# A modulation vector on four column strips of TensorE: norm1's part and g1 first, the rest in the course of the attention

## The chip, the cores and the metric

The kernel runs on one core of a Trainium2 chip. Its engines work side by side: TensorE (PE; its weight loads are listed as PEld), VectorE (DVE), ScalarE (ACT), GpSimd (POOL) and SyncE (SP, which here only issues DMAs). The metric is the device time of one execution in microseconds, lower is better. Times are given as the median of several runs, and one execution was recorded by the hardware profiler.

## The reference

One decoder layer over 1024 positions of width 1024. A vector c is turned into six rows of 1024 numbers, which shift, scale and gate the two sub-layers:

```python
c_act = jax.nn.silu(c)
mod = c_act @ ada_w[l] + ada_b[l]            # (1, 1024) @ (1024, 6144)
sh1, sc1, g1, sh2, sc2, g2 = jnp.split(mod, 6, axis=-1)
h = _rmsnorm(x, norm1_g[l]) * (1 + sc1) + sh1
p = h @ w_in[l]                              # q, k, v and u, 512 columns each
# q, k: RMS norm per head; 8 heads of 64, strictly causal stick-breaking attention
# u: 32 groups of a complex-diagonal state-space model (S5), gelu, GLU
o = concat(_rmsnorm(o_attn, attn_out_g[l]), _rmsnorm(o_ssm, ssm_out_g[l]))
x = x + g1 * (o @ w_out[l])
h = _rmsnorm(x, norm2_g[l]) * (1 + sc2) + sh2
up = causal_conv3(h @ ffn_w_up[l])           # width 2 * 2816
x = x + g2 * ((gelu(gate) * val) @ ffn_w_down[l])
```

The product with `ada_w` is a vector times a matrix of 1024 x 6144 in float32 (25 MB). It is what this change is about. Nothing else of the computation changes.

## The kernel before

The program is written out in full by Python loops, one instruction after another; a planner then orders each engine's instructions by a simulated timeline, so that instructions of one stage can stand between those of another, but each engine and each DMA queue then works strictly in the order given. Large products in float32 are done as three matmuls on rounded high and low halves (`hi`, `lo`).

Stages, in order:

1. norm1 and u (lines 141 to 238). For each of eight blocks k of 128 features, `load_k` fetches 1 MB of `ada_w` (the shift and the scale columns of that block, `ada_raw`) and the weights of u. The block's shift S1c and scale A1 come from the modulation; then x is transposed block by block on TensorE (line 233), ScalarE applies A1 and S1c (line 235), and `u_mm` adds the block to the projection of u. Five of its eight output tiles run inside the loop, the other three behind it (line 415). The modulation of block 0 is 16 matmuls with one column each (line 212); that of the other blocks is eight multiply-adds on VectorE over 256 columns (lines 215 to 217), whose 128 partitions a matmul with a column of ones then sums (line 220).
2. S5 and the projections of q, k and v (lines 412 to 650). `ssm_batch` runs four times between tiles of `proj`. Weight chunks of q, k and v are loaded and split by ScalarE and POOL (`load_wchunk`), into buffers which the chunk before must have left. `ada_back` (lines 560 to 583) computes six half rows of the modulation (g1, sh2, sc2), each with eight loads of 128x512 and eight multiply-adds on VectorE (line 569), and a sum over partitions on TensorE (line 573 or 577). It is a generator: `ada_step(3)` at line 601 advances it by three loads before each projection tile, and what is left is drained at line 649 behind the projection of v.
3. Attention (`head`, lines 679 to 726). Scores on TensorE (lines 697 to 700), two sigmoids on ScalarE (701, 702), a running product on VectorE (703), a product on POOL (705), transposes on TensorE (710), copies (714, 715) and the product with v (720, 721). Between the tiles, `after_tile` advances a second generator, `fillers`, at places given by the list `marks`, as shares of the heads' total weight: it prepares `w_out` (`wout_tile`, which multiplies by g1), and from mark 0.13 to 0.68 runs the output projection of the S5 half for eight row tiles (`ssm_out`, lines 795 to 799, a load of x, 24 matmuls and a store each). The buffers of `psM` in PSUM are shared by these. The last two heads run side by side when the fillers are done.
4. norm2 and the up projection (lines 894 to 1146), in 22 column blocks m; each `up_pair` is 84 matmuls of 512 columns. `g2_rows` computes a quarter of g2 behind each of the blocks 6 to 9, with eight loads and eight operations on VectorE each. g2 lies in the row that g1 had.
5. The down projection (lines 1158 to 1204), where the result is multiplied by g2.

The constants `ones` and `c_sb` (silu(c), one column per block of 128 inputs) are made at the start. All loads named here are issued from SP's queue.

Of the kernel before, what the change touches and what calls it, by code (L numbers as in the profile page):

```python
# [35 lines left out]
def hybrid_layer_kernel(  # L36
# [23 lines left out]
    def tt(eng, out, a, b, op):  # L60
        eng.tensor_tensor(out=out, in0=a, in1=b, op=op)  # L61
# [25 lines left out]
    cols_sb = const.tile([128, 32], F32, name="cols_sb")  # L87
    sp.dma_start(out=cols_sb, in_=cols)
    c_raw, n1g_sb, sh1b, sc1b = [cols_sb[:, 8 * i:8 * i + 8] for i in range(4)]
    cols2_sb = const.tile([128, 194], F32, name="cols2_sb")  # L90
    n2g_sb, outg_sb = cols2_sb[:, 0:8], cols2_sb[:, 8:16]
    cw_sb = cols2_sb[:, 16:148].rearrange("p (i m) -> p i m", i=3)
    cb_sb = cols2_sb[:, 148:192]
    gq_sb, gk_sb = cols2_sb[:, 192:193], cols2_sb[:, 193:194]

    ident = const.tile([128, 128], F32, name="ident")
    make_identity(nc, ident)
# [17 lines left out]
    o_d = dram.tile([512, 8, 128], F32, name="o_d")  # L115
    qk_d = dram.tile([2, 2, 512, 1024], F32, name="qk_d")
    x1_d = dram.tile([1024, 1024], F32, name="x1_d")
    x2_d = dram.tile([1024, 1024], F32, name="x2_d")
    a_d = dram.tile([NM * 128, 1024], F32, name="a_d")
    v_d = dram.tile([1024, 8, 128], F32, name="v_d")  # L120
# [80 lines left out]
    for k in range(NK):  # L201
        if k:
            load_k(k)
        if k == 1:
            sp.dma_start(out=cols2_sb, in_=cols2)
        raw = ada_raw[k]

        mps = psU.tile([128, 512], F32, tag="mps", name="mps", bufs=1)
        if k == 0:
            for i in range(2):  # L210
                for r in range(8):
                    pe.matmul(mps[:, i:i + 1], lhsT=raw[:, r, i * 128:(i + 1) * 128], rhs=c_sb[:, r:r + 1], start=(r == 0), stop=(r == 7))
        else:
            acc = pn.tile([128, 256], F32, tag="ada_acc", name="ada_acc1")
            dve.tensor_scalar(out=acc, in0=raw[:, 0, :], scalar1=c_sb[:, 0:1], scalar2=None, op0=MUL)
            for r in range(1, 8):
                stt(acc, raw[:, r, :], c_sb[:, r:r + 1], acc, MUL, ADD)
            for i in range(2):
                cs_ = slice(i * 128, (i + 1) * 128)
                pe.matmul(mps[:, i:i + 1], lhsT=acc[:, cs_], rhs=ones[:, 0:1], start=True, stop=True)  # L220
        tt(dve, S1c[:, k:k + 1], mps[:, 0:1], sh1b[:, k:k + 1], ADD)
        stt(A1[:, k:k + 1], mps[:, 1:2], sc1b[:, k:k + 1], n1g_sb[:, k:k + 1], ADD, MUL)
# [334 lines left out]

    TB, ZB, MB = 3, 2, 2

    def ada_back(ix):  # L560

        kind, o = divmod(ix * 512, 1024)
        acc = wp.tile([128, 512], F32, tag="uF", name="ada_acc", bufs=3)
        pool.memset(acc, 0.0)
        sp.dma_start(out=acc[0:1, :], in_=ada_br[ix:ix + 1, :])
        for r in range(8):
            raw = wp.tile([128, 512], F32, tag="uF", name="ada_raw", bufs=3)
            sp.dma_start(out=raw, in_=ada_r[ix, :, r])
            stt(acc, raw, c_sb[:, r:r + 1], acc, MUL, ADD)
            yield  # L570
        ps = psA.tile([128, 512], F32, tag="aux", name="adps")
        if kind == 0:
            pe.matmul(ps, lhsT=ones, rhs=acc, start=True, stop=True)
            act.activation(out=g1row[:, o:o + 512], in_=ps, func=AF.Copy)
        else:
            for j in range(4):
                pe.matmul(ps[:, j:j + 1], lhsT=acc[:, j * 128:(j + 1) * 128], rhs=ones[:, 0:1], start=True, stop=True)
            ks = slice(o // 128, o // 128 + 4)
            if kind == 1:
                act.activation(out=S2c[:, ks], in_=ps[:, 0:4], func=AF.Copy)  # L580
            else:
                stt(A2[:, ks], ps[:, 0:4], 1.0, n2g_sb[:, ks], ADD, MUL)
        yield

    ada_gen = (q for ix in range(6) for q in ada_back(ix))

    def ada_step(n):
        for _ in range(n):
# [3 lines left out]
    for cix in range(2):  # L592
        his, los = load_wchunk(cix)
        for tq in range(4):
# [3 lines left out]
            ssq = small.tile([128, 2, 8], F32, tag="qssq", name="qssq")  # L598
            inv = small.tile([128, 2, 8], F32, tag="qinv", name="qinv")
            for j in range(2):  # L600
                ada_step(3)
                o = proj(cix, tq * 2 + j, his, los)
                act.activation(out=qk[:, j].rearrange("p h d -> p (h d)"), in_=o, func=AF.Copy)
                ov = o.rearrange("p (h d) -> p h d", d=64)
                act.activation(out=o, in_=o, func=AF.Square)
                dve.tensor_reduce(out=ssq[:, j, :], in_=ov, op=ADD, axis=AX.X)  # L606
# [53 lines left out]
    osp = alloc("oprep", side="right", bufs=2)  # L660
    psZ, psT, psM = [alloc(n_, side=s_, bufs=1, space=PSUM) for n_, s_ in (("psZ", "right"), ("psT", "left"), ("psM", "left"))]
    ap_ = alloc("attn", bufs=2)
    vload = [None]

    def head_load_v(hd):
# [193 lines left out]
    for hd in range(NH):  # L859
        nxt = {}  # L860
        last_head = hd >= NH - 2

        def after_tile(i):
            if not last_head:
                if i == 0:
                    nxt["p"] = (after_v(head_load_qk, 1) if hd == 0 else head_load_qk(hd + 1), head_load_v(hd + 1))
            state["w"] += i + 2
            while state["q"] < len(marks) and marks[state["q"]] <= state["w"] / (44.0 * NH):
                state["q"] += 1
                with tc.issue_after(here[0].ins):  # L870
                    next(fill, None)

        if last_head:
            run_all(fill)
            load_xacc()
# [190 lines left out]
    g2row = g1row  # L1066
    uc = alloc("ffnconv", side="right")

    def g2_rows(q):

        ix, o = 6 + q // 2, (q % 2) * 256
        sl = slice(q * 256, (q + 1) * 256)
        sp.dma_start(out=g2row[:, sl], in_=ada_br[ix:ix + 1, o:o + 256].to_broadcast([128, 256]))
        acc = uc.tile([128, 256], F32, tag="g2acc", name="g2acc", bufs=1)
        for r in range(8):
            raw = uc.tile([128, 256], F32, tag="g2raw", name="g2raw", bufs=2)
            sp.dma_start(out=raw, in_=ada_r[ix, :, r, o:o + 256])
            if r == 0:
                dve.tensor_scalar(out=acc, in0=raw, scalar1=c_sb[:, 0:1], scalar2=None, op0=MUL)
            else:  # L1080
                stt(acc, raw, c_sb[:, r:r + 1], acc, MUL, ADD)
        ps = pools["D"].tile([128, 512], F32, tag="g2", name="adps2", bufs=1)
        pe.matmul(ps[:, 0:256], lhsT=ones, rhs=acc, start=True, stop=True)
        tt(dve, g2row[:, sl], ps[:, 0:256], g2row[:, sl], ADD)

    def up_operands(m):

        for r in range(2):
# [53 lines left out]
        conv(m, ups[m])  # L1142
    for m in range(FIRST, NM):
        up_pair(m)
        if 6 <= m < 10:
            g2_rows(m - 6)


    tp_.release()
# [66 lines left out]
def layouts(inputs):  # L1216
# [10 lines left out]
    r["cols"] = np.concatenate([col(a["c"][0]), col(a["norm1_g"][0]), col(adb[0]), col(adb[1])], axis=1)  # L1227
    r["cols2"] = np.concatenate([col(a["norm2_g"][0]), col(a["attn_out_g"][0]), col(a["ssm_out_g"][0]),
                                 col(a["ffn_conv_w"][0]), col(a["ffn_conv_b"][0]),
                                 twice(a["q_norm_g"][0]), twice(a["k_norm_g"][0])], axis=1)  # L1230
# [44 lines left out]
```

## Time and profile before

| | |
|---|---|
| median of 3 runs | 1327.32 us (1324.82 to 1327.82) |
| the profiled execution | 1323.88 us, its span 1322.0 us |
| busy in the span: PE, PEld | 1210.5 us (92%), 990.2 us (75%) |
| DVE | 1009.0 us (76%) |
| ACT, POOL | 586.6 us (44%), 477.4 us (36%) |
| mean granted TensorE clock | 0.957 of full speed |
| chain that ended last | PE 55%, DVE 27%, DMA 8%, issue 4%, ACT 3% |

Busy time is the time in which at least one instruction of the engine was under way. Matmuls are pipelined, so the next one starts before the last has ended: a busy TensorE is not one at its peak. In a line of the trace, "L212 PE MATMUL mps<-c_sb,ada_raw 128*128 128x1" is line 212 of the kernel on TensorE, writing tile mps from c_sb and ada_raw, with 128 rows and 128 columns of weights, and 128 partitions by 1 element of output; "[6.01 <-DVE Q L61]" is the idle time of that engine before it, and what ended it. Many operations go through helpers and so have a helper's line (61, 67, 160); they are told apart by the tiles.

### The profile page before, as it was taken

To read this page: it belongs to the slowest core of one execution; us is meant where nothing else is said; L and a number is where in the kernel's file an instruction comes from. 1 tells how busy PE (TensorE), PEld (TensorE's weight loads), DVE (VectorE), ACT (ScalarE), POOL (GpSimd) and SP (SyncE) were. 2 spreads that over 40 slices of the span, in tenths; PEclk is the share of its full clock that TensorE was granted. 3 is DMA by queue.
4 is the path that set the end of the run, shared out by engine and by line. 5 is a ranking of instruction groups with operands and counts; after the bars stand their busy time and mean duration, and the time that the engine had idled before them with its cause. 6 is when DMAs were issued, how large, how long until landed. Compare 5 with 4: busy or idle time off the path is not lost.

```text
span 1322.0 us, 16674 instructions
## 1 busy us (share of the span) xinstructions
PE 1210.5 (92%) x5752; PEld 990.2 (75%) x5752; DVE 1009.0 (76%) x1543; ACT 586.6 (44%) x1003; POOL 477.4 (36%) x367
## 2 busy tenths in 40 slices
PE   5879989989688996789998999999999999999998
PEld 4667768767567785678786887878888888888886
DVE  6999998984897899978897779778877773345334
ACT  5441333331484666637653544454545453223220
POOL 4462452430673358710044534445554510000000
PEclk9998989999788998889998999999999999999999
DMA  8452446558943774115033223222222155447442
GB/s 341 165 144 48 132 132 157 149 144 236 264 116 112 230 201 128 48 48 175 17 104 103 89 99 107 74 96 81 87 73 95 56 204 180 143 165 251 150 139 99
DMA packets 125631, 177.83 MB, mean 135 GB/s; under 512 B 36454, under 2 KB 73958, under 8 KB 124524
## 3 DMA queue, kind: packets, MB, share of 16 engines
q1 hardware_dynamic: 105484, 156.85, 37.7%
q10 hardware_dynamic: 20064, 19.93, 4.6%
q8 instruction: 45, 0.74, 0.2%
q14 instruction: 38, 0.31, 0.1%
HBM read 134.67 MB, written 40.89 MB: 133 GB/s over the span
## 4 chain that ended last, share of the span: by engine, by line
PE 55%; DVE 27%; DMA 8%; issue 4%; ACT 3%; POOL 1%; SPq 1%; ACTq 0%; DVEq 0%; POOLq 0%
PE dnps L1187 6%; PE dnps L1186 6%; PE dnps L1185 6%; PE up_a L991 5%; PE up_a L990 5%; PE up_a L992 5%; DVE ada_acc L67 4%; DMA ada_raw<-in_ada_r_dram 3%; DVE nb L703 3%; PE up_c L991 3%; PE up_c L992 3%; PE up_c L990 3%; PE wops L776 2%; PE wops L777 2%; PE wops L778 2%
## 5 line engine op out<-in xcount | busy, mean ns | idle before, releaser
L67 DVE SCALAR_TENSOR_TENSOR cv<-up,cols_sb,cv 128x1023 f32<-128x1023 f32 x88 | 137.6, 1565 | 15.8 <-ACT cv L1111 14.6
L61 DVE TENSOR_TENSOR alo<-araw,ahi 128x1024 fp32r<-128x1024 f32 x44 | 53.8, 1224 | 120.6 <-ACT ahi L160 120.5
L61 POOL TENSOR_TENSOR S<-upraw 128x512 f32<-128x512 f32 x40 | 70.2, 1756 | 208.0 <-DMA upraw<-in_w_up_dram 150.1
L1186 PE MATMUL dnps<-wdlo,ahi 128*128 128x512 f32 x352 | 136.9, 389 | 0.0
L1187 PE MATMUL dnps<-wdhi,alo 128*128 128x512 f32 x352 | 136.9, 389 | 0.0
L1185 PE MATMUL dnps<-wdhi,ahi 128*128 128x512 f32 x352 | 134.7, 389 | 0.0
L61 POOL TENSOR_TENSOR sig<-sig,nb 128x127 f32<-128x127 f32 (+3 forms) x64 | 100.6, 1583 | 65.6 <-DVE nb L703 44.5
L703 DVE TENSOR_TENSOR_SCAN nb<-nb 128x128 f32<-128x128 f32 (+3 forms) x64 | 108.8, 1712 | 4.5 <-ACT nb L701 4.2
L160 ACT ACTIVATE ahi<-araw 128x1024 fp32r<-128x1024 f32 x44 | 46.6, 1059 | 144.3 <-PE dnps L1186 128.0
L61 DVE TENSOR_TENSOR uplo<-S,uphi 128x512 fp32r<-128x512 f32 x80 | 90.5, 1136 | 19.7 <-ACT uphi L160 19.1
L61 POOL TENSOR_TENSOR cv<-cv 128x1024 f32<-128x1024 f32 x22 | 54.7, 2487 | 108.8 <-ACT cv L1115 99.3
L67 DVE SCALAR_TENSOR_TENSOR ada_acc<-ada_raw,c_sb,ada_acc 128x256 f32<-128x256 f32 (+1 forms) x97 | 73.4, 771 | 25.3 <-DMA ada_raw<-in_ada_r_dram 22.6
L160 ACT ACTIVATE uphi<-S 128x512 fp32r<-128x512 f32 x80 | 49.0, 625 | 89.6 <-POOL S L61 70.4
L553 PE MATMUL qkvp<-w_hi,hhi 128*128 128x512 f32 x192 | 78.4, 410 | 4.9 <-DVE qssq L606 2.9
L554 PE MATMUL qkvp<-w_lo,hhi 128*128 128x512 f32 x192 | 77.9, 406 | 0.8 <-POOL w_lo L61 0.8
L555 PE MATMUL qkvp<-w_hi,hlo 128*128 128x512 f32 x192 | 77.2, 402 | 0.0
L1186 PEld LDWEIGHTS dnps<-wdlo,ahi 128*128 128x128 f32 x352 | 66.1, 188 | 13.8
L1185 PEld LDWEIGHTS dnps<-wdhi,ahi 128*128 128x128 f32 x352 | 66.1, 188 | 13.7
L1187 PEld LDWEIGHTS dnps<-wdhi,alo 128*128 128x128 f32 x352 | 66.1, 188 | 13.6
L160 ACT ACTIVATE uphi<-upraw 128x512 fp32r<-128x512 f32 x68 | 41.5, 626 | 53.3 <-PE up_c L991 22.8
L710 PE MATMUL wT<-ident,sig 128*128 128x128 f32 x288 | 48.6, 294 | 18.0 <-DVE wl L61 10.1
L61 DVE TENSOR_TENSOR uplo<-upraw,uphi 128x512 fp32r<-128x512 f32 x68 | 60.0, 893 | 3.2 <-ACT uphi L160 3.2
(328 smaller groups left out, 3465.8 us busy)
## 6 DMA issues: line engine op xcount, KB each, us to landing
upraw<-in_w_up_dram SPq DMA_DIRECT2D x88, 256.0 KB, 3.0
araw<-a_d SPq DMA_DIRECT2D x44, 512.0 KB, 3.4
ada_raw<-in_ada_r_dram SPq DMA_DIRECT2D x48, 256.0 KB, 3.0
a_d<-cv ACTq DMA_DIRECT2D x22, 512.0 KB, 2.6
wdraw<-in_w_down_dram SPq DMA_DIRECT2D x44, 256.0 KB, 3.5
ada_raw<-in_ada_a_dram SPq DMA_DIRECT2D x8, 1024.0 KB, 9.5
qk_d<-hl ACTq DMA_DIRECT2D x32, 256.0 KB, 3.0
q<-qk_d SPq DMA_DIRECT2D x32, 256.0 KB, 6.2
```

The costliest lines, as they stand in the source:

```text
L61: eng.tensor_tensor(out=out, in0=a, in1=b, op=op)
L67: dve.scalar_tensor_tensor(out=out, in0=a, scalar=s, in1=b, op0=op0, op1=op1)
L160: act.activation(out=o, in_=i, func=AF.Copy)
L553: pe.matmul(o, lhsT=lh, rhs=his[k], start=(k == 0), stop=False)
L554: pe.matmul(o, lhsT=lh, rhs=los[k], start=False, stop=False)
L703: dve.tensor_tensor_scan(out=nb[:, 0:n][:, ::-1], data0=nb[:, 0:n][:, ::-1], data1=nb[:, 0:n][:, ::-1], initial=1.0, op0=MUL, op1=ALU.bypass)
L990: pe.matmul(ps, lhsT=hi[:, kt, :], rhs=rh, start=(first and kt == 0), stop=False, skip_group_check=True)
L991: pe.matmul(ps, lhsT=hi[:, kt, :], rhs=rl, start=False, stop=False, skip_group_check=True)
L992: pe.matmul(ps, lhsT=lo[:, kt, :], rhs=rh, start=False, stop=(kt == 3), skip_group_check=True)
L1185: pe.matmul(o[t], lhsT=hi[:, a], rhs=whi, start=(m == 0), stop=False)
L1186: pe.matmul(o[t], lhsT=hi[:, a], rhs=wlo, start=False, stop=False)
L1187: pe.matmul(o[t], lhsT=lo[:, a], rhs=whi, start=False, stop=(m == NM - 1))
```

## The change

The product now goes through TensorE with c as the weights. `c32` holds silu(c) copied to 32 columns for each of the eight input blocks, and `mean32` is a 128x128 matrix of 1/32. For a piece of `ada_w`, eight matmuls (one for each input block) write the four strips of 32 partitions of one PSUM tile, two input blocks adding up in each strip; ScalarE copies the tile to SBUF, and one more matmul with `mean32` sums the strips, which divides the 32 copies out. Norm1's eight blocks do this on 256 columns, for block 0 as for the others. The other 4096 columns go in 32 jobs of 128 columns, each with two loads of 128x4x128 (512 bytes in a run): eight jobs for g1, one before each projection tile, and 24 for sh2, sc2 and g2 at marks of their own in the attention, with PSUM tiles of `psM`. g2 is stored to DRAM row by row and loaded again, broadcast to 128 partitions, at block 11 of the up projection; `g2_rows` is gone. The biases of sh2 and sc2 come with `cols2`.

```diff
+    c32 = hp.tile([128, 8, 32], F32, name="c32")
+    dve.tensor_copy(c32, c_sb.unsqueeze(2).to_broadcast([128, 8, 32]))
+    mean32 = hp.tile([128, 128], F32, name="mean32")
+    pool.memset(mean32, 1.0 / 32.0)
+    def strips(ps, raw, h, hs):
+        for i in range(4):
+            pe.matmul(ps[32 * i:32 * i + 32], lhsT=c32[:, h * 4 + i, :], rhs=raw[:, i, :], start=(h == 0), stop=(h == 1))
...
-        if k == 0:
-            for i in range(2):
-                for r in range(8):
-                    pe.matmul(mps[:, i:i + 1], lhsT=raw[:, r, i * 128:(i + 1) * 128], rhs=c_sb[:, r:r + 1], start=(r == 0), stop=(r == 7))
-        else:
-            acc = pn.tile([128, 256], F32, tag="ada_acc", name="ada_acc1")
-            dve.tensor_scalar(out=acc, in0=raw[:, 0, :], scalar1=c_sb[:, 0:1], scalar2=None, op0=MUL)
-            for r in range(1, 8):
-                stt(acc, raw[:, r, :], c_sb[:, r:r + 1], acc, MUL, ADD)
...
+        for h_ in range(2):
+            strips(mps[:, 0:256], raw[:, h_ * 4:h_ * 4 + 4, :], h_, 2)
+        acc = pn.tile([128, 256], F32, tag="ada_acc", name="ada_acc1")
+        act_copy(acc, mps[:, 0:256])
+        for i in range(2):
+            pe.matmul(mps[:, 256 + i:257 + i], lhsT=acc[:, i * 128:(i + 1) * 128], rhs=mean32[:, 0:1], start=True, stop=True)
...
+    def ada_back(pl, tags, ps_new, consts, ixs):
+        cw, mean = consts
+        jobs = [(ix, c) for ix in ixs for c in range(4)]
...
+        load(0)
+        yield
+        for n, (ix, c) in enumerate(jobs):
+            kind, o = divmod(ix * 512 + c * 128, 1024)
+            ps = ps_new("adps")
+            for r in range(8):
+                i = r % 4
+                pe.matmul(ps[32 * i:32 * i + 32, 0:128], lhsT=cw[:, r, :], rhs=raws[2 * n + r // 4][:, i, :], start=(r < 4), stop=(r >= 4))
+            load(n + 1)
+            acc = pl.tile([128, 128], F32, tag=tags[1], name="ada_acc", bufs=1)
+            act_copy(acc, ps[:, 0:128])
+            if kind in (0, 3):
+                row = g1row[:, o:o + 128] if kind == 0 else pl.tile([128, 128], F32, tag="adarow", name="g2", bufs=1)[0:1, :]
+                src = ada_br[ix:ix + 1, c * 128:(c + 1) * 128]
+                sp.dma_start(out=row, in_=src.to_broadcast([128, 128]) if kind == 0 else src)
+                pe.matmul(ps[:, 128:256], lhsT=mean, rhs=acc, start=True, stop=True)
+                tt(dve, row, ps[0:row.shape[0], 128:256], row, ADD)
+                if kind == 3:
+                    sp.dma_start(out=g2_d[ix - 6:ix - 5, c * 128:(c + 1) * 128], in_=row)
+            else:
+                pe.matmul(ps[:, 128:129], lhsT=acc, rhs=mean[:, 0:1], start=True, stop=True)
...
-    ada_gen = (q for ix in range(6) for q in ada_back(ix))
+    ada_gen = ada_back(wp, ("uF", "adacc", 3), lambda nm: psA.tile([128, 512], F32, tag="aux", name=nm), (c32, mean32), range(2))
...
-                ada_step(3)
+                ada_step(1)
...
+    ada_fill = ada_back(ap_, ("adaw", "adacc", 2), psB_new, (c32b, mean32b), range(2, 8))
+    ada_marks = [0.04 + 0.62 * j / 25 for j in range(25)]
...
+            while ada_marks and ada_marks[0] <= state["w"] / (44.0 * NH):
+                ada_marks.pop(0)
+                with tc.issue_after(here[0].ins):
+                    next(ada_fill, None)
...
-        if 6 <= m < 10:
-            g2_rows(m - 6)
+        if m == NM // 2:
+            for i in range(2):
+                sp.dma_start(out=g2row[:, i * 512:(i + 1) * 512], in_=g2_d[i:i + 1, :].to_broadcast([128, 512]))
```

## Rows read from the trace of the kernel before

**Rows 1.** Windows: length; PE, PEld, DVE, ACT, POOL busy (instructions); PEclk, DMA share, GB/s
```profile
0.00:20.00 20.00, 7.91 (x36) 7.54 (x36) 7.56 (x30) 12.87 (x21) 5.99 (x19) 1.00 0.92 358
20.00:91.00 71.00, 63.94 (x280) 49.75 (x280) 70.59 (x218) 32.96 (x57) 43.39 (x33) 0.93 0.52 174
...
104.00:303.00 199.00, 182.75 (x997) 147.51 (x996) 178.47 (x334) 60.15 (x95) 78.11 (x65) 0.94 0.49 131
303.00:332.40 29.40, 28.76 (x128) 23.16 (x128) 10.20 (x15) 3.59 (x6) 2.35 (x8) 1.00 0.86 256
...
337.40:405.00 67.60, 49.75 (x250) 38.45 (x251) 63.11 (x67) 47.74 (x102) 53.04 (x40) 0.80 0.65 179
405.00:505.00 100.00, 95.07 (x559) 79.43 (x557) 84.16 (x115) 62.83 (x143) 39.46 (x54) 0.98 0.63 195
...
660.00:735.00 75.00, 68.56 (x284) 55.48 (x284) 62.92 (x72) 35.75 (x52) 28.66 (x15) 0.95 0.31 102
...
856.00:1046.00 190.00, 188.95 (x834) 156.01 (x833) 152.71 (x141) 94.22 (x140) 99.05 (x52) 1.00 0.23 81
```

**Rows 2.** Windows, tiles ada_acc (two) and g2acc (last): PE, PEld, DVE, then POOL for ada_acc
```profile
20.00:91.00 71.00, 4.51 (x28) 4.44 (x28) 31.94 (x56) 0.00 (x0) 0.93 0.52 174
104.00:337.40 233.40, 6.47 (x36) 5.07 (x36) 44.39 (x48) 2.63 (x5) 0.95 0.53 145
...
660.00:856.00 196.00, 2.37 (x8) 1.50 (x8) 26.97 (x32) 0.98 0.29 97
```

**Rows 3.** Timeline of TensorE (matmuls, weight loads): start, us, instruction, xcount [idle before]
```profile
11.29 6.96 PE L212 MATMUL mps<-c_sb,ada_raw 128*128 128x1 f32 x32 [11.29 <-DVE inv L67]
...
211.95 1.97 PE L490 MATMUL vps<-U,W 128*64 128x128 f32 x32
213.84 0.42 PEld L615 LDWEIGHTS qkT<-ident,qk 128*128 128x128 f32 x4 [0.17 <-issue]
...
292.65 1.50 PE L524 MATMUL gps<-ys,G 128*128 128x128 f32 x12
```

**Rows 4.** Groups by form (busy us, mean ns); L490 (min/median/max ns); a wait (us, times, longest)
```profile
L490 PE MATMUL vps<-U,W x128: 272/273/477, 106.5 to 257.2; 128*64 128x128 f32 x128
...
L1083 PE MATMUL adps<-g2acc,ones 128*128 128x256 f32 x8 | 2.4, 378 | 0.0
...
L714 ACT ACTIVATE wh<-wT 128x128 fp32r<-128x128 f32 x16 | 4.6, 289 | 3.2 <-PE wT L710 3.1
...
L61 DVE TENSOR_TENSOR blk<-kp,dd 128x128 f32<-128x128 f32 x4 | 1.1, 282 | 0.0
...
PE nps L758 <- DVE otot L757: 5.1, 5, 3.3
```

**Rows 5.** Timeline of TensorE behind u, and at the start of the attention
```profile
97.08 1.12 PE L464 MATMUL w1p<-ident,Q 128*128 128x128 f32 x4 [6.01 <-DVE Q L61]
...
331.85 0.39 PE L555 MATMUL qkvp<-w_hi,hlo 128*128 128x512 f32 x1
336.13 1.41 PE L577 MATMUL adps<-ones,ada_acc 128*128 128x1 f32 x8 [3.89 <-issue]
337.40 0.45 PE L697 MATMUL z<-k,q 128*128 128x128 f32 x1
```

**Rows 6.** Timeline of SP's queue: the first and the last of eight loads of x
```profile
400.54 0.33 SPq L797 DMA_DIRECT2D x<-in_x_dram  x1
...
486.20 0.34 SPq L797 DMA_DIRECT2D x<-in_x_dram  x1
```

**Rows 7.** Timeline of VectorE: three of the 22 additions of up_b, and a g2 operation
```profile
704.90 0.48 DVE L67 SCALAR_TENSOR_TENSOR g2acc<-g2raw,c_sb,g2acc 128x256 f32<-128x256 f32 x1 [1.88 <-DMA g2raw<-in_ada_r_dram]
...
735.25 0.68 DVE L61 TENSOR_TENSOR up<-up_b,up 128x512 f32<-128x512 f32 x1
...
855.94 0.68 DVE L61 TENSOR_TENSOR up<-up_b,up 128x512 f32<-128x512 f32 x1
...
1046.35 0.68 DVE L61 TENSOR_TENSOR up<-up_b,up 128x512 f32<-128x512 f32 x1
```

More of the change, by code (lines that the diff above doesn't have):

```diff
@@ L89, in hybrid_layer_kernel @@
     c_raw, n1g_sb, sh1b, sc1b = [cols_sb[:, 8 * i:8 * i + 8] for i in range(4)]
-    cols2_sb = const.tile([128, 194], F32, name="cols2_sb")
+    cols2_sb = const.tile([128, 210], F32, name="cols2_sb")
     n2g_sb, outg_sb = cols2_sb[:, 0:8], cols2_sb[:, 8:16]
@@ L94, in hybrid_layer_kernel @@
     gq_sb, gk_sb = cols2_sb[:, 192:193], cols2_sb[:, 193:194]
+    sh2b, sc2b = cols2_sb[:, 194:202], cols2_sb[:, 202:210]
     ident = const.tile([128, 128], F32, name="ident")
@@ L117, in hybrid_layer_kernel @@
     x1_d = dram.tile([1024, 1024], F32, name="x1_d")
+    g2_d = dram.tile([2, 512], F32, name="g2_d")
     x2_d = dram.tile([1024, 1024], F32, name="x2_d")
@@ L208, in hybrid_layer_kernel @@
         mps = psU.tile([128, 512], F32, tag="mps", name="mps", bufs=1)
-        if k == 0:
-            for i in range(2):
-                for r in range(8):
-                    pe.matmul(mps[:, i:i + 1], lhsT=raw[:, r, i * 128:(i + 1) * 128], rhs=c_sb[:, r:r + 1], start=(r == 0), stop=(r == 7))
-        else:
-            acc = pn.tile([128, 256], F32, tag="ada_acc", name="ada_acc1")
-            dve.tensor_scalar(out=acc, in0=raw[:, 0, :], scalar1=c_sb[:, 0:1], scalar2=None, op0=MUL)
-            for r in range(1, 8):
-                stt(acc, raw[:, r, :], c_sb[:, r:r + 1], acc, MUL, ADD)
[L218 to L222, printed above, removed]
+        for h_ in range(2):
[4 more added lines that the diff above has]
+            pe.matmul(mps[:, 256 + i:257 + i], lhsT=acc[:, i * 128:(i + 1) * 128], rhs=mean32[:, 0:1], start=True, stop=True)
+        tt(dve, S1c[:, k:k + 1], mps[:, 256:257], sh1b[:, k:k + 1], ADD)
+        stt(A1[:, k:k + 1], mps[:, 257:258], sc1b[:, k:k + 1], n1g_sb[:, k:k + 1], ADD, MUL)
         hi = wp.tile([128, 512], F32R, tag="whi", name="wu_hi", bufs=8)
@@ L558, in hybrid_layer_kernel @@
     TB, ZB, MB = 3, 2, 2
[L560 to L569, printed above, removed]
-            yield
[L571 to L583, printed above, removed]
@@ L585, in hybrid_layer_kernel, with load @@
-    ada_gen = (q for ix in range(6) for q in ada_back(ix))
+    def ada_back(pl, tags, ps_new, consts, ixs):
+        cw, mean = consts
+        jobs = [(ix, c) for ix in ixs for c in range(4)]
+        raws = []
+        def load(n):
+            if n < len(jobs):
+                ix, c = jobs[n]
+                for h_ in range(2):
+                    raw = pl.tile([128, 4, 128], F32, tag=tags[0], name="ada_raw", bufs=tags[2])
+                    sp.dma_start(out=raw, in_=ada_r[ix, :, h_ * 4:h_ * 4 + 4, c * 128:(c + 1) * 128])
+                    raws.append(raw)
+        load(0)
[19 more added lines that the diff above has]
+                pe.matmul(ps[:, 128:129], lhsT=acc, rhs=mean[:, 0:1], start=True, stop=True)
+                ks = slice(o // 128, o // 128 + 1)
+                if kind == 1:
+                    tt(dve, S2c[:, ks], ps[:, 128:129], sh2b[:, ks], ADD)
+                else:
+                    tt(dve, A2[:, ks], ps[:, 128:129], sc2b[:, ks], ADD)
+                    stt(A2[:, ks], A2[:, ks], 1.0, n2g_sb[:, ks], ADD, MUL)
+            yield
@@ L662, in hybrid_layer_kernel @@
     ap_ = alloc("attn", bufs=2)
+    c32b = ap_.tile([128, 8, 32], F32, name="c32b", bufs=1)
+    dve.tensor_copy(c32b, c_sb.unsqueeze(2).to_broadcast([128, 8, 32]))
+    mean32b = ap_.tile([128, 128], F32, name="mean32b", bufs=1)
+    pool.memset(mean32b, 1.0 / 32.0)
     vload = [None]
@@ L874, in hybrid_layer_kernel @@
             run_all(fill)
+            run_all(ada_fill)
             load_xacc()
@@ L1067, in hybrid_layer_kernel @@
     uc = alloc("ffnconv", side="right")
[L1069 to L1084, printed above, removed]
     def up_operands(m):
@@ L1229, in layouts @@
                                  col(a["ffn_conv_w"][0]), col(a["ffn_conv_b"][0]),
-                                 twice(a["q_norm_g"][0]), twice(a["k_norm_g"][0])], axis=1)
+                                 twice(a["q_norm_g"][0]), twice(a["k_norm_g"][0]),
+                                 col(adb[3]), col(adb[4])], axis=1)
     r["ada_a"] = ada[:, :, 0:2].reshape(8, 128, 2, 8, 128).transpose(3, 1, 0, 2, 4).reshape(8, 128, 8, 256)
```

## The prediction

> **What bounds the kernel now.** I read the table of stages first, then the modulation's own busy time, then the rows at each edge. In the table [rows 1] compare the PE and DVE columns line by line. From 20 to 91 us (norm1 and the projection of u) VectorE is busy 70.59 of 71 us and TensorE 63.94: VectorE is the bound, TensorE close behind. From 104 to 303 (S5 batches, q, k and the first v tiles) it is 178.47 and 182.75 of 199. From 303 to 332.4 TensorE alone is full. From 337.4 to 405 (first heads) VectorE is busy 63.11 of 67.6 and TensorE 49.75; from 405 to 505 TensorE 95.07 of 100. From 856 to 1046 (up projection) TensorE is busy 188.95 of 190. So an edit that moves work from VectorE to TensorE pays in front and costs in the later heads.
>
> Next the modulation itself [rows 2]: it holds VectorE 31.94 us between 20 and 91, 44.39 us between 104 and 337.4, and 26.97 us between 660 and 856, 103.3 us of its 1009. In the first of these it is 45% of what the bounding engine does.
>
> **Part 1, one product in strips.** Each product becomes eight matmuls with 32 columns of weights. A float32 matmul here is two instructions (32 for line 212's 16 calls [rows 3]), so 16 instructions. Undivided 128x128 ones follow each other every (1.50 - 0.27)/11 = 0.112 us; those on two halves of the columns every (1.97 - 0.27)/31 = 0.055 us [rows 3]. Halves overlap by two; quarters I don't see. Bounds for a 128-wide product: 16 x 0.112 = 1.79 us if quarters take turns, 16 x 0.027 = 0.44 us if all four overlap. I take the nearest row, 0.055: 0.87 us. For 256 columns an instruction streams twice as long (0.378 against 0.273 us, where the difference is those 128 more columns [rows 4]), so 1.75 us, with bounds 0.87 and 3.5. Then a copy on ScalarE (0.29 us for 128x128) and a float32 mean of two instructions (0.22 us), and on VectorE an operation of 0.28 us at most [rows 4]. Going in and out of strips: after the 32 half matmuls the next weight load came after 0.17 us [rows 3]. Sum on TensorE: 0.87 + 0.22 + 0.17 = 1.26 us for 128 columns, bounds 0.83 and 2.18.
>
> The Trainium skill speaks against strips here: "TensorEngine Tiling (Array Packing)", Key Properties, says that a change of tiling mode drains the engine. The trace agrees to the extent of that 0.17 us; no row shows a longer drain. With it as a cost of each of 40 entries, the page adds nothing to the sum above.
>
> **Part 2, norm1 (to 104 us).** VectorE loses 31.94 us of work and is no longer last. TensorE gains 8 x 1.75 = 14 us and loses the 6.96 us of line 212 [rows 3]: 7 us more. That fits into its 71 - 63.94 = 7.1 us of idle time and the 5 us that a granted clock of 0.93 cost there [rows 1], so u ends where it did. TensorE is next late, not VectorE; ScalarE, busy 33 of 71, hides the copies. What goes is the gap behind u: TensorE idles 6.01 us at 97 for an operand that VectorE had not got to [rows 5], because 32 us of modulation stood ahead of it. Value -6. Bounds: -14 (all four strips overlap, 7 us less) and +8 (in turns: 28 - 7 = 21 us, less 12 of slack).
>
> **Part 3, the rows in the projections (104 to 337.4).** 48 multiply-adds go (44.39 us); g1 alone stays, in 8 products. TensorE: 8 x 1.26 = 10 us in, 6.47 us of old reductions out of [rows 2], of which 1.41 lie in the tail. The tail is sure: v's last matmul starts at 331.85, then TensorE idles 3.89 us for the last modulation row, 1.41 us go to it, and the first head starts at 337.40 [rows 5]. The loads that feed it stand on SP's queue between the stores of v; both go. -5. In the body TensorE idles 199 - 182.75 = 16 us and loses 0.06 x 199 = 12 us to the granted clock of 0.94 [rows 1]. I take half of these 28 back, as VectorE sinks to some 70% busy; the other half I leave to changes of weight chunk, which wait on splits by POOL that nothing here moves. 14 - 5 = 9. Together -14; bounds -26 (nearly all comes back) and +2 (only the tail, strips in turns).
>
> **Part 4, 24 products in the attention.** The new marks run from 0.04 to 0.66 of the heads' weight. The old filler's marks 0.13 to 0.68 are the eight loads of x, issued from 400.54 to 486.20 us [rows 6], so three products fall before 400 us and 21 between 400 and 500, where TensorE is full. 21 x 1.26 = 26.5 us, less 4.9 us of idle time and 2 us of slow clock [rows 1]: +19. The three early ones hide in 17.9 idle us. VectorE and ScalarE get 24 x 0.28 = 7 us each: both have 15 and more us free between 405 and 505. DMA: 21 x 0.5 MB in 95 us are 116 GB/s on 195; the 358 GB/s of the first 20 us bound that [rows 1], so the loads fit. On SP's queue a load stands behind the release of its two buffers by the strips before; behind it wait q, k, v and x of what comes, loaded a head ahead (x has one buffer). On TensorE the mean stands behind ScalarE's copy; behind it stand the scores. Bounds: +4 (0.83 each, part of it in start-up times that the busy column hides) and +45 (2.18 each, nothing hidden).
>
> **Part 5, g2 out of the up projection.** 26.97 us of VectorE go. The pace shows what that is worth: from 856 to 1046 without g2 ten column blocks take 190.41 us, 19.04 each; from 735 to 856 with g2 six take 120.69, 20.12 each [rows 7]. Six times 1.08 are 6.5 us. Between 660 and 735 TensorE idles 6.4 us and loses 3.8 to the clock [rows 1], with VectorE standing for a g2 row at 704.90 for 1.88 us [rows 7]; I give 3.5 of it to g2. -10; bounds -12 and -5. The two broadcast loads that replace it are needed only by the down projection, over 200 us later, and cost nothing.
>
> **Sum.** -6 - 14 + 19 - 10 = -11. The profiled execution took 1323.88 us (its span 1322.0 and 1.9 around it), so 1313; the median of the three runs lies 3.4 us above that execution, so I forecast 1316.
>
> **The rivals.** First, all four strips overlap. For it: halves gain exactly their factor of two (0.055 against 0.112). Against: both instructions of a call go to one strip, back to back, so at most the end of one and the start of the next may overlap. Then norm1 gains 7 more, the projections 3.5, and the heads 21 x 0.43 = 9: -11 - 19.5 = -30, 1297. The skill's page on tiling gives this rule too (Theoretical Speedup: up to 4 times for a dimension of 32 or less); no run here shows it yet.
>
> Second, slower: the attention pays for every product in waits. Place: TensorE between strips and mean, in order, with the scores behind it. Price: the reduction that stands likewise behind another engine, nps, waited 5.1 us in 5 waits [rows 4], 1.0 us each. 24 x (1.26 + 1.0) = 54 us with no slack used: -6 - 14 + 54 - 10 = +24, 1351. It decides from 30 us on in the heads, that is from 0.5 us of wait per product. For it: each wait holds a full engine. Against: the order is planned ahead, and scores and transposes can stand in between.
>
> Third, the front is held by TensorE and weight chunks, not by VectorE: parts 2 and 3 shrink to the tail's 5 us, which the eight products eat. 0 + 0 + 19 - 10 = +9, 1336. For it: TensorE is 90% busy there already. Against: the 6.01 us and the clock.
>
> That the change doesn't do what it says: strips that take turns, the upper bounds above; with them +8, +2, +45, -10 make +45. The halves' row speaks against it; it shares the second rival's chance.
>
> **How the numbers follow.** Forecast 0.45 (own range 1303 to 1328), first rival 0.22, second 0.2, third 0.13. Low: the forecast and the first rival down to 1288. High: 1342, into the second rival. Faster or slower by 0.2%, 2.7 us, is about what a measurement of this kernel can tell from no change: below 1324.6 lie the first rival, nine tenths of the forecast and a part of the third, 0.64; within, 0.08; above, 0.28.
>
> **What would show it.** Right: strip instructions 0.05 to 0.06 us apart at 128 columns and 0.11 at 256; VectorE under 75% between 20 and 300 us; the first score 15 to 25 us before 337; from there to the end of the heads 15 to 25 us more than the 253 us of 337.4 to 590; about 19.1 us per column block all through. Wrong: a front that ends where it ended (third rival), TensorE idle before the means or the scores behind them (second), strips 0.03 us apart (first), or attention no longer than before, which would mean that 95% busy had room I did not see.

## The result, and the profile after

The changed kernel takes 1318.42 us (median of 10 runs, 1311.39 to 1324.17), against 1327.38 us before (10 runs, 1324.82 to 1327.82): a ratio of 0.9927, 95% interval 0.9911 to 0.9943, or 9.0 us. The forecast was 1316. The profiled execution of the changed kernel took 1319.42 us, its span 1317.6, so the two traces differ by 4.4 us and the medians by 9.0.

First the head of its page: span, busy time, and the chain of waits.

```profile
span 1317.6 us, 17825 instructions
...
PE 1227.3 (93%) x6384; PEld 996.6 (76%) x6384; DVE 945.9 (72%) x1443; ACT 602.0 (46%) x1039; POOL 462.0 (35%) x363
...
PE 73%; DVE 14%; DMA 5%; POOL 3%; ACT 3%; issue 2%; SPq 0%; ACTq 0%; DVEq 0%; POOLq 0%
```

VectorE has 63 us less work, TensorE 17 us more, and TensorE now makes up 73% of the chain, where it was 55%. The windows by stage answer to [rows 1] (columns as there); those of the attention start at the first score as there, and the last is moved with its stage.

```profile
20.00:91.00 71.00, 65.01 (x379) 48.71 (x379) 57.27 (x239) 34.30 (x60) 36.53 (x30) 0.95 0.51 176
96.60:295.00 198.40, 189.56 (x1157) 154.06 (x1157) 145.51 (x283) 64.95 (x105) 73.05 (x63) 0.96 0.46 117
...
316.00:383.60 67.60, 51.40 (x333) 40.98 (x334) 58.76 (x69) 48.95 (x108) 49.87 (x40) 0.80 0.76 207
383.60:483.60 100.00, 91.28 (x689) 72.66 (x687) 76.17 (x123) 56.45 (x135) 37.99 (x50) 0.95 0.75 208
...
660.00:735.00 75.00, 72.12 (x305) 57.90 (x304) 63.99 (x69) 42.66 (x64) 30.48 (x17) 0.95 0.21 71
852.00:1042.00 190.00, 190.00 (x835) 156.46 (x834) 162.24 (x139) 95.65 (x138) 100.10 (x51) 1.00 0.24 81
```

In front VectorE falls from 70.59 to 57.27 of 71 us and from 178.47 of 199 to 145.51 of 198.4, and TensorE fills up. But in the heads, where the products were added, TensorE is *less* busy than before: 91.28 of 100 us against 95.07 [rows 1]. More work and less of the engine used means new waits.

The edges of the stages, on TensorE's timeline of the changed kernel (start, us, instruction): the last operations ahead of the projections, the first projection matmul, the first score, the first transpose of norm2, the first matmul of the down projection.

```profile
94.06 1.03 PE L472 MATMUL w1p<-ident,Q 128*128 128x128 f32 x8
94.93 1.87 PE L478 MATMUL kp<-cpair,Q 128*128 128x32 f32 x16
96.64 0.48 PE L561 MATMUL qkvp<-w_hi,hhi 128*128 128x512 f32 x1
...
315.99 0.33 PE L727 MATMUL z<-k,q 128*128 128x128 f32 x1 [1.41 <-DVE vt L61]
...
606.71 0.82 PE L983 MATMUL tp<-ident,xn 128*128 128x128 f32 x6
...
1073.51 0.39 PE L1206 MATMUL dnps<-wdhi,ahi 128*128 128x512 f32 x1
```

The same edges of the kernel before; its first score is at 337.40 [rows 5].

```profile
103.64 0.77 PE L553 MATMUL qkvp<-w_hi,hhi 128*128 128x512 f32 x1
...
598.07 0.81 PE L946 MATMUL tp<-ident,xn 128*128 128x128 f32 x6
...
1077.48 0.39 PE L1185 MATMUL dnps<-wdhi,ahi 128*128 128x512 f32 x1
```

Subtracting edge from edge: the front loses 21.4 us (337.4 to 316.0), 7 of them ahead of the projections; the attention from the first score to norm2 gains 30.0 (260.7 to 290.7); norm2 and the up projection lose 12.6 (479.4 to 466.8); the rest stays. The forecast had -20, +19 and -10. So the sum was near, and one stage was off by 11 us. The experiments were mostly about that stage.

### The profile page after: what moved, and what is told of

The parts are those of the page before. It is cut to its first block, busy times and chain, and to the rows that moved or that the text cites. A ratio compares the mean times of both kernels' runs of the same rounds, so it can differ in the third digit from the quotient of the medians.

```text
span 1317.6 us, 17825 instructions
## 1 busy us (share of the span) xinstructions
PE 1227.3 (93%) x6384; PEld 996.6 (76%) x6384; DVE 945.9 (72%) x1443; ACT 602.0 (46%) x1039; POOL 462.0 (35%) x363
## 4 chain that ended last, share of the span: by engine, by line
PE 73%; DVE 14%; DMA 5%; POOL 3%; ACT 3%; issue 2%; SPq 0%; ACTq 0%; DVEq 0%; POOLq 0%
PE dnps L1206 6%; PE dnps L1207 6%; PE dnps L1208 6%; PE up_a L1028 6%; PE up_a L1029 6%; PE up_a L1027 6%; PE up_c L1028 3%; PE up_c L1029 3%; PE up_c L1027 3%; PE wops L806 2%; PE qkvp L563 2%; PE wops L807 2%; PE qkvp L562 2%; PE qkvp L561 2%; PE wops L808 2%
## 5 line engine op out<-in xcount | busy, mean ns | idle before, releaser
L67 DVE SCALAR_TENSOR_TENSOR cv<-up,cols_sb,cv 128x1023 f32<-128x1023 f32 x88 | 145.6, 1655 | 20.5 <-ACT cv L1131 19.8
L61 POOL TENSOR_TENSOR S<-upraw 128x512 f32<-128x512 f32 x40 | 75.6, 1891 | 181.9 <-DMA upraw<-in_w_up_dram 139.5
L61 POOL TENSOR_TENSOR sig<-sig,nb 128x127 f32<-128x127 f32 (+3 forms) x64 | 90.8, 1428 | 94.2 <-DVE nb L733 49.3
L61 DVE TENSOR_TENSOR uplo<-S,uphi 128x512 fp32r<-128x512 f32 x80 | 98.1, 1228 | 26.9 <-ACT uphi L174 25.8
L733 DVE TENSOR_TENSOR_SCAN nb<-nb 128x128 f32<-128x128 f32 (+3 forms) x64 | 102.9, 1617 | 9.7 <-ACT nb L731 9.3
L1207 PEld LDWEIGHTS dnps<-wdlo,ahi 128*128 128x128 f32 x352 | 66.1, 188 | 13.6
L61 DVE TENSOR_TENSOR uplo<-upraw,uphi 128x512 fp32r<-128x512 f32 x68 | 68.5, 1009 | 1.6 <-ACT uphi L174 1.6
L806 PE MATMUL wops<-wohi,ohi 128*128 128x512 f32 x128 | 54.1, 427 | 6.8 <-POOL wohi L177 3.7
```

Of the source, the lines that this page charges most:

```text
L67: dve.scalar_tensor_tensor(out=out, in0=a, scalar=s, in1=b, op0=op0, op1=op1)
L1207: pe.matmul(o[t], lhsT=hi[:, a], rhs=wlo, start=False, stop=False)
```

## The experiments

A time "against before" is the median minus that of the kernel before in runs on the same chip. By that measure the change itself is -9.0. "Heads" is the time from the first score to norm2's first transpose in the profiled execution.

**Without the products in the attention.**

```diff
-    ada_marks = [0.04 + 0.62 * j / 25 for j in range(25)]
+    ada_marks = []
+    act_copy(S2c, sh2b)
+    stt(A2, sc2b, 1.0, n2g_sb, ADD, MUL)
+    sp.dma_start(out=g2_d, in_=ada_br[6:8, :])
...
-            run_all(ada_fill)
```

> The changed kernel without the 24 products in the attention: norm2's shift and scale and g2 are taken from the bias rows alone, so the modulation by c is left out of them. The time gives the price of all 24. Theory A (the products hold PSUM tiles that the filler matmuls of the attention need, so that the fillers run late and w_out is split late): heads and tail from the first score to norm2's first transpose lose the 30 us that they gained, 290.7 to about 261, and the time is about 1288. Theory B (the products cost TensorE only their own time, 24 x 1.26 us less idle time, the +19 of the prediction): 1299. Theory C (the strips overlap by four, 24 x 0.83 us less idle time): 1308.

Measured: 1299.67 us (5 runs, 1293.82 to 1302.68), ratio 0.979 (0.9769 to 0.9812), -27.0 against before. The 24 products cost 27.0 - 9.0 = 18.0 us: theory B's number, and close to the prediction's 19. But the heads did not go back to 260.7:

```profile
316.72 0.33 PE L727 MATMUL z<-k,q 128*128 128x128 f32 x1 [1.41 <-DVE vt L61]
...
587.63 0.82 PE L985 MATMUL tp<-ident,xn 128*128 128x128 f32 x6
```

270.9 us, 10 more than before, with none of the products in it. So the +30 is some 20 of products and 10 of something else.

**PSUM tiles.** Three runs: the products in a tile of their own at the expense of one transpose tile, the control that only gives up the transpose tile, and the products in the three transpose tiles.

```diff
 # own tile; the control has the first edit alone
-    TB, ZB, MB = 3, 2, 2
+    TB, ZB, MB = 2, 2, 2
-    ada_fill = ada_back(ap_, ("adaw", "adacc", 2), psB_new, (c32b, mean32b), range(2, 8))
+    ada_fill = ada_back(ap_, ("adaw", "adacc", 2), lambda nm: psM.tile([128, 512], F32, tag="ada", name=nm, bufs=1), (c32b, mean32b), range(2, 8))
 # in the transposes' tiles: TB stays 3, psB_new is replaced by
+    lambda nm: psT.tile([128, 512], F32, tag="T", name=nm, bufs=TB)
```

> The changed kernel, but its 24 products in the attention have a PSUM tile of their own; one of the transposes' three tiles is given up for it. To be read against e4, which gives up the same tile and changes nothing else. Theory A (shared PSUM tiles hold the fillers back): at least 10 us faster than e4, and the last x of ssm_out is stored before 515 us rather than at 536. Theory B (TensorE's own time for the products): within 3 us of e4, last store unmoved.

> Control for e3: the changed kernel with two PSUM tiles for transposes instead of three, the products still in the tiles of the fillers. Both theories: slower than the changed kernel by what a transpose tile is worth, 0 to 15 us, 1318 to 1333.

> The changed kernel with the 24 products taking one of the transposes' three PSUM tiles in turn, instead of one of the fillers' two; nothing else changes. Theory A: the fillers no longer alternate with the products, so the time falls by 5 to 20 us, to 1298 to 1313, unless transposes wait for products in the same way (then it rises). Theory B: 1318, within 3 us.

Measured: own tile 1319.03 us, ratio 0.9949 (0.9935 to 0.9963); control 1326.59, 1.0002 (0.9984 to 1.002); transposes' tiles 1328.4, 1.0013 (1.0001 to 1.0026). A transpose tile is worth 8.9 us, a tile for the products 7.6: sharing costs something, less than theory A's 10 and more than B's 3. In the transposes' tiles the products made the kernel 10.7 us slower than the change, the exception that theory A had named. The trace shows a part of it: TensorE's transposes waited 5.5 us for the copy `wl` that reads such a tile last, 2.9 in the changed kernel, and its products 1.6. The trace of the own tile takes theory A's second half down: x's last store came at 497.6 us, not at 536, `w_out` was in time, and yet the heads took 289.3 us (315.50 to 604.81). Late `w_out` was not the reason.

What the traces show instead is VectorE standing in front of x's additions. Groups of VectorE in the attention (instruction, forms, count | busy, mean ns | idle before, and what ended it): first the kernel before, then the changed one, then the one with an own tile, then that without products.

```profile
L67 DVE SCALAR_TENSOR_TENSOR x<-wops,sinv,x 128x512 f32<-128x512 f32 x16 | 11.5, 736 | 8.8 <-PE z L700 5.9 <-DMA x<-in_x_dram 2.8
```

```profile
L67 DVE SCALAR_TENSOR_TENSOR x<-wops,sinv,x 128x512 f32<-128x512 f32 x16 | 11.9, 748 | 20.2 <-PE wops L808 19.5 <-DMA x<-in_x_dram 0.5 <-PE z L728 0.2
```

```profile
L67 DVE SCALAR_TENSOR_TENSOR x<-wops,sinv,x 128x512 f32<-128x512 f32 x16 | 11.7, 743 | 18.8 <-DMA x<-in_x_dram 15.3 <-PE wops L808 3.5
```

```profile
L67 DVE SCALAR_TENSOR_TENSOR x<-wops,sinv,x 128x512 f32<-128x512 f32 x16 | 11.6, 738 | 15.4 <-DMA x<-in_x_dram 10.7 <-PE z L730 3.0 <-PE wops L808 1.7
```

Read the idle time: 8.8 us before, 20.2, 18.8 and 15.4 after. Then read what ended it. With an own tile and without products most of it ended with a load of x (15.3 and 10.7 us; 2.8 before). In the changed kernel 19.5 of the 20.2 us ended with TensorE's output projection (`wops`) and only 0.5 with a load of x. The longest of these waits began at TensorE, with a product whose load was late (TensorE, TensorE, VectorE):

```profile
446.87 0.66 PE L589 MATMUL adps<-ada_raw,c32b 128*32 128x128 f32 x8 [3.34 <-DMA ada_raw<-in_ada_r_dram]
447.45 0.80 PE L806 MATMUL wops<-wohi,ohi 128*128 128x512 f32 x1
...
452.82 0.75 DVE L67 SCALAR_TENSOR_TENSOR x<-wops,sinv,x 128x512 f32<-128x512 f32 x1 [7.79 <-PE wops L808]
```

Behind the 3.34 us of idle time the granted clock was 0.50 from 447.4 to 452.3 us, 1.2 instead of 2.4 GHz, and the twelve matmuls for the addition came every 0.43 us, where those before came every 0.23. So two things can hold an addition: the load of x, and TensorE.

As to the load: x has one buffer in SBUF. A row tile is loaded, takes two additions, is stored, and only then can the next be loaded. VectorE works in order, so what stands behind an addition, the running products of the heads, stands too. SP's queue in the changed kernel shows the cycle (L829 stores x, L827 loads the next, L579 loads for a product):

```profile
413.51 0.34 SPq L829 DMA_DIRECT2D x_d<-x  x1
415.77 0.92 SPq L579 DMA_DIRECT2D ada_raw<-in_ada_r_dram  x2
417.27 0.34 SPq L827 DMA_DIRECT2D x<-in_x_dram  x1
417.71 0.38 SPq L697 DMA_DIRECT2D vsb<-v_d  x1
419.26 8.60 SPq L579 DMA_DIRECT2D ada_raw<-in_ada_r_dram  x4
431.34 0.34 SPq L829 DMA_DIRECT2D x_d<-x  x1
...
434.34 0.58 SPq L827 DMA_DIRECT2D x<-in_x_dram  x1
```

Product loads stand between a store and the next load. The one load of x whose landing this trace tells took 7.5 us; before, three tell: 3.4, 3.4 and 4.8. One row tile takes 17 us here; the eight loads of x run from 386.0 to 524.8 us, 19.8 each, against (486.20 - 400.54)/7 = 12.2 before [rows 6]. On SP's timelines most of the difference lies between a load and its store (15.4 us on average, 9.5 before), where TensorE's output projection and the additions stand; from a store to the next load it is 3.9 against 2.9.

**Norm1 alone, and g2 alone,** to price parts 2 and 5 by themselves on the kernel before.

```diff
 # norm1 alone: the change's norm1 edit, nothing else (its strips are shown)
+        for h_ in range(2):
+            strips(mps[:, 0:256], raw[:, h_ * 4:h_ * 4 + 4, :], h_, 2)
...
 # g2 alone
-        if 6 <= m < 10:
-            g2_rows(m - 6)
+        if m == NM // 2:
+            for i in range(2):
+                sp.dma_start(out=g2row[:, i * 512:(i + 1) * 512], in_=ada_br[6 + i:7 + i, :].to_broadcast([128, 512]))
```

> The kernel before with norm1's products alone done in strips; everything from the projections on stays as it was. The prediction's part 2: u and the projections start 6 us earlier (bounds -14 to +8), and the whole kernel gains it: 1320. Rival (TensorE holds the front): 1326 or more. Second theory, from the first experiment, where the attention without any product still took 10 us longer than before (270.9 against 260.7 us from the first score to norm2's first transpose): a front that ends earlier is partly paid back in the attention, whose order of instructions comes out differently: first score 6 us or more earlier, but half of it gone by norm2, 1323 to 1325.

> The kernel before with g2 taken from its bias row alone (the modulation of g2 by c is left out of the computation): VectorE's 26.97 us in the up projection go and nothing takes their place. The prediction's part 5: -10 us (bounds -12 to -5), 1316 to 1317; norm2's first transpose where it was, the pace about 19.1 us per column block all through. Rival (VectorE's work there was hidden): within 3 us of before.

Measured: norm1 alone 1321.77 us, ratio 0.9975 (0.9956 to 0.9994), -4.6; -6 was forecast, the interval is -5.8 to -0.8 us. Its 12 runs spread from 1318.96 to 1330.28, and the profiled one was among the longest (1328.99), so its stages say little: its first projection matmul came 1.1 us earlier than before (102.58), at a granted clock of 0.88 from 97 to 303 us, where [rows 1] have 0.94. Whether the gain lies at the front, and how much of it the attention took back, can't be told from it. Without g2 1312.77 us, ratio 0.9893 (0.9873 to 0.9914), -13.6: more than the forecast 10 and the bound of 12. By edges norm2 and the up projection take 465.0 us (601.18 to 1066.18), 14.4 less than before. Of the surplus, the window from 660 to 735 shows a part: TensorE busy 73.81 us, 68.56 before [rows 1], 5.2 us more, where I had given g2 3.5.

```profile
660.00:735.00 75.00, 73.81 (x311) 60.56 (x312) 64.60 (x64) 39.59 (x57) 35.22 (x19) 0.95 0.23 77
```

**Two buffers for x,** without the products and on the kernel before.

```diff
-        xt_ = osp.tile([128, 1024], F32, tag="x1", name="x1", bufs=1)
+        xt_ = osp.tile([128, 1024], F32, tag="x1", name="x1", bufs=2)
```

(the tag's other tiles, `woraw` and `junk2`, likewise)

> The first experiment's kernel (no products in the attention; the modulation of norm2 and g2 by c left out) with two SBUF buffers for x in the attention instead of one. In that experiment VectorE stood 10.7 us for loads of x, against 2.8 us in the kernel before. Theory X (the single buffer of x is what lengthened the attention by 10 us): 5 to 10 us faster than that experiment's 1299.67, about 1291, and the last x stored before 475 us instead of at 483.5. Theory O (the order of instructions as a whole, many small waits): within 3 us of 1300.

> The kernel before with two SBUF buffers for x in the attention instead of one and no other change: the control for the run with two buffers and no products. Theory X: VectorE stood only 2.8 us for loads of x, so 0 to 3 us faster, 1324 to 1327. Theory O: within 3 us as well, either way.

Measured: without the products 1280.63 us, ratio 0.9656 (0.9632 to 0.968), 18.7 us less than with one buffer; on the kernel before 1324.65, ratio 0.9985 (0.997 to 1.0), 1.7 less. The same edit is worth 18.7 us in the new order and 0 to 4 in the old, by the interval. So the attention in its new order did want for a buffer, as theory X had it, and theory X's 5 to 10 us were too few. That the gain comes by x alone is not shown, since the tag has other tiles: without products the last load of `w_out` is issued at 490.6 us with two buffers and at 542.2 with one. VectorE's idle time in front of x, without the products:

```profile
L67 DVE SCALAR_TENSOR_TENSOR x<-wops,sinv,x 128x512 f32<-128x512 f32 x16 | 11.7, 735 | 2.8 <-PE wops L808 2.8
...
317.14 0.33 PE L727 MATMUL z<-k,q 128*128 128x128 f32 x1 [1.41 <-DVE vt L61]
...
570.60 0.81 PE L985 MATMUL tp<-ident,xn 128*128 128x128 f32 x6
```

and in the kernel before with two buffers, both with the edges of the heads on TensorE:

```profile
L67 DVE SCALAR_TENSOR_TENSOR x<-wops,sinv,x 128x512 f32<-128x512 f32 x16 | 11.8, 738 | 2.0 <-PE wops L778 1.9
...
338.76 0.45 PE L697 MATMUL z<-k,q 128*128 128x128 f32 x1
...
600.66 0.82 PE L946 MATMUL tp<-ident,xn 128*128 128x128 f32 x6
```

In the first it fell by 12.6 us (from 15.4) and the heads by 17.4 (270.9 to 253.5); in the second by 6.8 (from 8.8), and the heads did not get shorter (260.7 and 261.9). So this idle time alone does not set the length; what else held the kernel before is not shown.

**The changed kernel with more buffers, and with the products elsewhere.** The four load buffers take memory that lies idle until the up projection, which makes room for x's second buffer.

```diff
 # four load buffers
+                    raw = (us if tags[0] == "S" else pl).tile([128, 4, 128], F32, tag=tags[0], name="ada_raw", bufs=tags[2])
...
+        if tags[0] == "S":
+            load(1)
...
+            load(n + (2 if tags[0] == "S" else 1))
+    ada_fill = ada_back(ap_, ("S", "adacc", 4), psB_new, (c32b, mean32b), range(2, 8))
 # other places; the drain moves behind the last two heads
-    ada_marks = [0.04 + 0.62 * j / 25 for j in range(25)]
+    ada_marks = [0.0] + [0.02 + 0.1 * j / 8 for j in range(8)] + [0.14 + 0.5 * j / 8 for j in range(8)] + [0.7 + 0.26 * j / 8 for j in range(8)]
```

> The changed kernel with the loads of its 24 products in four SBUF buffers (memory that lies idle until the up projection), two products ahead instead of one. TensorE stood 7.3 us for these loads in the attention. Theory X (the single buffer of x holds the attention back): at most that, 1311 to 1318. Theory L (late loads are what the products cost): 10 us or more, 1308 or less.

> The kernel with four load buffers, and x in the attention in two buffers instead of one. Theory X: what two buffers gave without products (19 us) comes here too, 1293 to 1303, and the last x is stored well before 500 us instead of at 536. Theory P (x runs late in the changed kernel because it and the products take turns at the two PSUM tiles): within 5 us of the kernel with four load buffers alone.

> The changed kernel with its 24 products at other places: 8 of them in the first eighth of the attention, where TensorE was busy 44.8 of 60 us, 8 along x, and g2's 8 in the last two heads, where it was busy 50.3 of 71 us; the buffers are as in the changed kernel. If the products' price is TensorE's time (18.75 us for 24): the 16 that are moved to where it idles save 5 to 12 us, 1306 to 1313. If the chain of the heads through VectorE and GpSimd sets the pace there (VectorE busy 37.3 of 40 us from 536 to 576): no gain or a loss, 1317 to 1326.

> Four load buffers, x in two buffers, and the 24 products at the other places (8 in the first eighth, 8 along x, 8 in the last two heads) together. If both help: 5 to 12 us below the kernel with x in two buffers. If the places don't matter or hurt: the same or above.

Measured: four load buffers 1313.56 us, ratio 0.9894 (0.9873 to 0.9916); with x in two buffers 1300.28, 0.9788 (0.9764 to 0.9812); other places alone 1313.1, 0.9886 (0.9862 to 0.991); all together 1296.93, 0.9773 (0.9753 to 0.9792). Earlier loads give 4 us (-13.1 against -9.0, with intervals that just overlap), the second buffer 13.3 more: theory X's time, not that of theories L and P. The places give 4.6 alone, just under what was expected; on top of the buffers 3.4, also under it, with intervals that overlap, so that is open. In front of x, with four load buffers, VectorE stood

```profile
L67 DVE SCALAR_TENSOR_TENSOR x<-wops,sinv,x 128x512 f32<-128x512 f32 x16 | 11.9, 746 | 19.7 <-PE wops L810 6.9 <-DMA x<-in_x_dram 6.1 <-issue 3.6
```

and with x in two buffers besides

```profile
L67 DVE SCALAR_TENSOR_TENSOR x<-wops,sinv,x 128x512 f32<-128x512 f32 x16 | 12.0, 748 | 8.7 <-PE wops L810 8.5
```

11.0 us less, of which 6.1 had ended with a load of x, and the heads 283.3 (312.18 to 595.52) and 271.1 (314.19 to 585.31), 12.2 less. x's last store came at 512.2, not "well before 500": again it is not how late x ends that counts. The last version, 1296.93 us, beats the kernel before by 29.8 us and the changed one by 20.8.

## Why the prediction was right, and where it was not

**The sum** (-11, 1316) was right within 2.4 us; by medians its terms measure -4.6 (norm1), +18.0 (products) and -13.6 (g2), and by edges of the traces -14.4 for the projections (21.4 less the 7 ahead of them). That makes -14.6, while the whole is -9.0: some 5.6 us are given back by a term that the prediction didn't have, the heads' loss without products, which is 10 us in the two traces. That the sum came so near all the same is in part luck: the spans of the two traces differ by 4.4 us, not by 11, and only the medians differ by 9.0.

**Part 2, norm1.** -6 against -4.6. The step held in kind: the gap behind u (6.01 us [rows 5]) is gone, w1p starts at 94.06 without idle time, and from the end of u to the first projection matmul it is 2.6 us, where it was 12.6. "u ends where it did" did not hold: it ended at 97.08 - 6.01 = 91.07 and now ends at 94.06. VectorE's share between 20 and 300 us, forecast under 75%, is 73% (205.09 of 280); in norm1 alone it is 81% (57.27 of 71). The bound +8 should have been +9 (21 less 12).

```profile
20.00:300.00 280.00, 265.17 (x1593) 211.91 (x1593) 205.09 (x525) 101.68 (x169) 113.39 (x96) 0.96 0.47 133
```

**Part 3, the projections.** -14 against -14.4. The tail went as foreseen: the first score starts 1.8 us after v's last matmul (314.19 on the timeline), where it took 337.40 - 331.85 = 5.55 [rows 5]. The third rival, a front held by TensorE, is out.

**Part 1, the strip.** The mis-sized step. TensorE's timeline of the changed kernel, one product of 256 columns, one of 128, and one of 128 in two halves:

```profile
28.13 1.07 PE L145 MATMUL mps<-ada_raw,c 128*32 128x256 f32 x16 [0.26 <-PE tp L241]
...
131.98 0.64 PE L589 MATMUL adps<-ada_raw,c 128*32 128x128 f32 x16
132.55 0.50 PE L563 MATMUL qkvp<-w_hi,hlo 128*128 128x512 f32 x1
...
364.15 0.43 PE L589 MATMUL adps<-ada_raw,c32b 128*32 128x128 f32 x8 [0.27 <-DMA ada_raw<-in_ada_r_dram]
364.94 0.43 PE L589 MATMUL adps<-ada_raw,c32b 128*32 128x128 f32 x8 [0.37 <-DMA ada_raw<-in_ada_r_dram]
```

At 128 columns the 16 instructions follow each other every (0.64 - 0.27)/15 = 0.025 us, at 256 every (1.07 - 0.38)/15 = 0.046 (single ones last 0.27 and 0.38 [rows 4]). I had 0.055 and 0.11: all four strips overlap, and undivided ones come every 0.112. That is the first rival's mechanism, by the sign that I had named for it. The factor of up to four for a dimension of 32 or less is the one that the Trainium skill states ("TensorEngine Tiling (Array Packing)", Theoretical Speedup). The trace agrees: 0.112/4 = 0.028, near the 0.025 measured. My argument against it, that the two instructions of a call go to one strip, was wrong. The 0.17 us for the switch does show: 16 steps of 0.025 are 0.40 us, and the next matmul starts 0.57 us after the first strip. Still the first rival's 1297 did not come: norm1 and the projections, at -4.6 and -14.4, did not gain its further 7 and 3.5 us, and the product in the attention is more than its strips:

```profile
L589 PE MATMUL adps<-ada_raw,c32b 128*32 128x128 f32 x384 | 18.6, 291 | 9.3 <-DMA ada_raw<-in_ada_r_dram 7.3 <-DVE x L67 1.3 <-DVE S2c L61 0.7
L602 PE MATMUL adps<-mean32b,ada_acc 128*128 128x1 f32 x32 | 5.1, 230 | 0.0
L597 PE MATMUL adps<-ada_acc,mean32b 128*128 128x128 f32 x16 | 3.4, 297 | 0.0
```

These are TensorE's groups in the attention: strips 18.6 us (0.78 each, not 0.64, mainly since 11 of the 24 products run in two halves of 0.43 us each), means 8.5, together 27.1/24 = 1.13 us a product, where I had 1.26; and 9.3 us of idle time in front of the strips, 7.3 for loads.

**Part 4, the heads.** +19 against 18.0 for the products, and +30 for the stage. The price was right, in part by luck: less TensorE time than I took (27.1 against 30.2 us for 24) and waits for loads that I took as free ("the loads fit": by bandwidth they do, 208 GB/s in the window from 383.6, but a load issued one product ahead came late, worth 4 us by the run with four buffers). The second rival, TensorE between strips and mean, is out: the idle time before both means is 0.0. The stage's +30 does touch the mark that the prediction set for this rival, but only 18 to 20 of it are the products'. What failed is the step that noted x's one buffer and gave it no price. In the order that came out of this change a second buffer for x's tag is worth 13.3 us with the products and 18.7 without, against 1.7 in the kernel before. By which wait it acts is shown only in part: without products 10.7 us of VectorE's idle time in front of x ended with loads of x, in the changed kernel 0.5.

Why the heads without products take 10 us more than before in the first place, I can only narrow down: much the same instructions in another order, and the second buffer takes away more than the 10. That a planner that starts the attention 21 us earlier makes such an order by necessity was not shown.

**Part 5, g2.** -10 against -13.6 alone and -12.6 in the changed kernel: right in kind; the stretch from 660 to 735 was given too little. The pace of about 19.1 us per column block came: from the sixth addition of up_b to the twenty-first it is (1042.48 - 755.38)/15 = 19.14 in the changed kernel.

```profile
755.38 0.68 DVE L61 TENSOR_TENSOR up<-up_b,up 128x512 f32<-128x512 f32 x1
...
1042.48 0.68 DVE L61 TENSOR_TENSOR up<-up_b,up 128x512 f32<-128x512 f32 x1
```

## What to carry to other kernels

When a change moves work into a stage that is nearly full, look for the buffers there that are single and in a cycle (load, use, store, load): such a buffer was worth 2 us here in one order of the instructions and 13 to 19 us in another, and one more buffer tells. A stage that gets more work and shows its bounding engine less busy has new waits. Look where another engine stands (here VectorE, in front of x's additions), and then at what ended each wait: the same idle time ended with a load in one version and with TensorE in another. Price a moved part by leaving it out: the 24 products cost what was forecast, so the rest of the stage's loss had to be something else.

## What the runs showed of the hardware that was not expected

Four strips of 32 columns overlap in full in float32, two instructions to a call: one instruction every 0.025 us at 128 columns and 0.046 at 256, and the next undivided matmul up to 0.17 us late behind them. Behind one wait of TensorE for a load, 3.34 us, the granted clock was 0.50 over the next 4.9 us, and matmuls came every 0.43 us instead of every 0.23. A transpose tile in PSUM, the third of three, was worth 8.9 us in the attention.
